# First SwiGLU products of a transformer trunk: four of seven products chained through one PSUM bank, two products issued with 512-column matmuls

## The chip, the cores and the metric

One core of a Trainium2 chip runs the kernel. Its five engines run their own instruction streams and wait for each other through semaphores: PE (matmuls, with weight loads shown as PEld), DVE (VectorE), ACT (ScalarE), POOL (GpSimd, here mostly an issuer of transfers) and SP (another issuer of transfers). The metric is the time of one execution in device microseconds; lower is better.

## The reference

Two layers, each with two SwiGLU blocks around a token mixer. What the change touches is the first product of each SwiGLU block (and the sums of its input), four blocks in all:

```python
D_MODEL, SEQ, DEPTH, D_FF = 1024, 512, 2, 2816

def swiglu(x, w13, w2):
    a, b = jnp.split(x @ w13, 2, axis=-1)
    return (jax.nn.silu(a) * b) @ w2

for l in range(DEPTH):
    x = layer_norm(ALPHA * x + 0.5 * swiglu(x, ffn1_w13[l], ffn1_w2[l]), ...)
    x = layer_norm(ALPHA * x + mixer(x, ...), ...)
    x = layer_norm(ALPHA * x + 0.5 * swiglu(x, ffn2_w13[l], ffn2_w2[l]), ...)
```

Everything is float32. The kernel keeps that precision by splitting each operand into a high and a low part (`split`: ACT writes the high part rounded to fp32r, L126; DVE writes the remainder, L127) and issuing three matmuls for each tile: high x high, high x low, low x high.

## The kernel before, in words

`x @ w13` has 22 column tiles of 128 for `a` and 22 for `b`. Tiles k and k + 11 of `a` and of `b` form a "pair" k, and of the 11 pairs ten (0 to 9) are computed by `seven_pairs`. There the 512 tokens are cut into two halves of 256, the 1024 input features into two halves of 512, and the 2 x 2 x 2 block product is done with seven block products in place of eight, on sums of blocks. So there are sums of input blocks (`x_sums`, once for each SwiGLU: s1 to s4) and sums of weight blocks (`PairWeights.sum`, L570, DVE, four for each pair: t, b, c and a are overwritten or filled by sums of the raw blocks a, b, c, d).

A product is 2 column tiles (z) x 4 feature tiles (m) x 3 matmuls = 24 matmuls of 256 columns (L590). `ORDER` lists the seven products: accumulating bank, input block, weight block. The loop over n = 7 * pair + product does, for each n, in this order: the first part of the eviction of product n - 1 from its bank, a weight sum, the split (L126, L127) of the weights of product n + 3, the rest of the eviction, and in pairs 1, 2, 4, 5, 7 and 8 behind product 3 the sums and splits of an earlier pair's results (`activation_sums`, L337 to L341), and then the matmuls of product n. Every ACT and DVE instruction of this is pinned, so each of these two engines gets its instructions in exactly the order of the code; PE's order is set by a scheduler that may move a matmul ahead of another that waits. Below, "heavy" pair means one with `activation_sums`, "light" pair one without.

Each pair has four PSUM banks of 128 x 512, out of eight. Before, they are A, C, E and B. The evictions of `evictions(k, m)` (L603 to L622) hold three ACT copies or Silu out of PSUM, an ACT Silu in SBUF, and seven 512-wide DVE operations.

```python
ORDER = (("A", "A11", "a"), ("C", "s1", "t"), ("A", "A12", "c"), ("E", "s3", "b"), ("B", "s2", "a"),
         ("C", "s4", "d"), ("E", "A22", "c"))
AHEAD = 3
```

Split weights live in ten buffers, five high and low pairs. The rest of a SwiGLU (`Seven.run`, the second product, 512-column matmuls), the mixer and the norms are not changed, except that the sign of the input sum s2 turns and the parts of the sums lie otherwise in memory.

Of the kernel before, what the change touches and what calls it, by code (L numbers as in the profile page):

```python
# [28 lines left out]
F32 = mybir.dt.float32  # L29
F32R = mybir.dt.float32r  # L30
I32 = mybir.dt.int32
AF = mybir.ActivationFunctionType
# [3 lines left out]
P = 128  # L36
# [47 lines left out]
def trunk(ctx: ExitStack, tc, x_in, xt_in, w13, w2, w_in, w_iv, w_br, w_out, ln_g, ln_b, lb_in, hgn, sgg, sgb, sgws,  # L84
# [12 lines left out]
    def bank(name):  # L97
        return psum.tile([P, 512], F32, tag="ps", name=name)
# [21 lines left out]
    def pin(ins):  # L120

        if pinned[0]:
            tc.keep_in_program_order(ins)

    def split(hi, lo, src):
        pin(S.activation(hi, src, AF.Copy))  # L126
        pin(V.tensor_tensor(lo, src, hi.bitcast(F32), op=ALU.subtract))  # L127
# [145 lines left out]
    def quads(name, dtype=F32):  # L273
        return slot(name, dtype).rearrange("p a t -> p (a t)").rearrange("p (q t) -> p q t", q=4)
# [224 lines left out]
    def x_sums(s, gap=X_GAP):  # L499

        lo_t, hi_t = slice(0, 256), slice(256, 512)
        x3 = quads("xs3")
        v = {c: [] for c in ("s1", "s2", "s3", "s4")}
        for q in range(2):
            r, r2 = xr[q], xr[q + 2]
            v["s1"].append(r[:, :, hi_t])
            v["s2"].append(r2[:, :, hi_t])
            v["s3"].append(x3[:, 2 * q:2 * q + 2])
            v["s4"].append(r2[:, :, lo_t])
            V.tensor_tensor(v["s3"][q], r[:, :, lo_t], r[:, :, hi_t], op=ALU.subtract)  # L510
            V.tensor_tensor(v["s1"][q], r[:, :, hi_t], r2[:, :, hi_t], op=ALU.subtract)
        firsts = [xr[q][:, :, lo_t] for q in range(2)]

        def parts(c):
            s[c] = tuple(quads(f"x{c}{z}", F32R) for z in "hl")
            for q in range(2):
                split(s[c][0][:, 2 * q:2 * q + 2], s[c][1][:, 2 * q:2 * q + 2], v[c][q])

        parts("s1")
        yield 0.0, gap  # L520
        parts("s3")
        for q in range(2):
            V.tensor_tensor(v["s2"][q], firsts[q], v["s1"][q], op=ALU.subtract)
        yield 0.0, gap
        parts("s2")
        for q in range(2):
            V.tensor_tensor(v["s4"][q], v["s4"][q], v["s2"][q], op=ALU.subtract)
        yield 0.0, gap
        parts("s4")


    ORDER = (("A", "A11", "a"), ("C", "s1", "t"), ("A", "A12", "c"), ("E", "s3", "b"), ("B", "s2", "a"),
             ("C", "s4", "d"), ("E", "A22", "c"))
    AHEAD = 3

    class PairWeights:
# [35 lines left out]
    def seven_pairs(seven, s, ks, weights_of, first, due):  # L572


        half = slice(0, 256), slice(256, 512)
        movs = {"A11": lambda m: (xh[m // 2][:, m % 2, half[0]], xl[m // 2][:, m % 2, half[0]]),
                "A12": lambda m: (xh[2 + m // 2][:, m % 2, half[0]], xl[2 + m // 2][:, m % 2, half[0]]),
                "A22": lambda m: (xh[2 + m // 2][:, m % 2, half[1]], xl[2 + m // 2][:, m % 2, half[1]])}
        for c in s:
            movs[c] = lambda m, c=c: (s[c][0][:, m], s[c][1][:, m])  # L580

        def product(ps, units, c, first):
            for z in range(2):
                hi, lo = units[0][:, z], units[1][:, z]
                for m in range(4):
                    ms = slice(m * P, (m + 1) * P)
                    mh, ml = movs[c](m)
                    for i, (a, v) in enumerate(((hi, mh), (hi, ml), (lo, mh))):
                        start = first and z == 0 and m == 0 and i == 0
                        PE.matmul(ps[:, half[z]], a[:, ms], v, start=start, stop=(m == 3 and i == 2),  # L590
                                  skip_group_check=not (first and z == 0))
                    flow.tick(3 * 120.0)

        pws = {ks[0]: first}
        at = lambda n: (ks[n // 7], n % 7)
        last = 7 * len(ks)
        banks = {}

        def evictions(k, m):
            b, r = banks[k], seven.room(k).rearrange("p q t -> p (q t)")  # L600
            lower, upper = r[:, 0:512], r[:, 512:1024]
            if m == 0:
                pin(S.activation(upper, b["A"], AF.Copy))  # L603
            elif m == 2:
                pin(S.activation(lower, b["A"], AF.Silu))
            elif m == 1:
                b["b1"] = wk.tile([P, T], F32, tag="sa", name="b1", bufs=NSA)
                pin(S.activation(b["b1"], b["C"], AF.Copy))
            elif m == 3:
                pin(V.tensor_tensor(b["b1"], b["b1"], b["E"], op=ALU.subtract))  # L610
            elif m == 4:
                pin(V.tensor_tensor(upper, upper, b["B"], op=ALU.subtract))
                pin(V.tensor_tensor(b["b1"], b["b1"], upper, op=ALU.subtract))
            elif m == 5:
                b0 = wk.tile([P, T], F32, tag="sa", name="b0", bufs=NSA)
                pin(V.tensor_tensor(b0, b["C"], upper, op=ALU.subtract))
                pin(V.tensor_tensor(lower, lower, b0, op=ALU.mult))
            elif m == 6:
                pin(V.tensor_tensor(upper, b["E"], upper, op=ALU.add))
                yield  # L620
                pin(S.activation(upper, upper, AF.Silu))
                pin(V.tensor_tensor(upper, upper, b["b1"], op=ALU.mult))  # L622

        for n in range(last):
            k, m = at(n)
            nk = at(n + 7)[0] if n + 7 < last else None
            if m == 0 and nk is not None:
                pws[nk] = weights_of(nk)
                pws[nk].load_d()
            elif m == 1 and nk is not None:  # L630
                pws[nk].load_c()
            ev = evictions(*at(n - 1)) if n else iter(())
            next(ev, None)
            if m == 0:
                banks[k] = {c: bank(f"f{c}{k}") for c in "ABCE"}
                pws[k].sum("a", "a", "b")
            elif m == 1:
                pws[k].sum("c", "a", "c")
            elif m == 2 and nk is not None:
                pws[nk].sum("t", "a", "b")  # L640
            elif m == 3 and nk is not None:
                pws[nk].sum("b", "d", "b")
            if n + AHEAD < last:
                pws[at(n + AHEAD)[0]].split()
            for _ in ev:
                pass
            if m == 3:
                for v in due.get(k, ()):
                    seven.activation_sums(v)
            c, mov, _ = ORDER[m]  # L650
            product(banks[k][c], pws[k].parts[m], mov, c == "B" or m in (0, 1, 3))
        for _ in evictions(*at(last - 1)):
            pass

# [7 lines left out]
    def ffn(l, i, first, next_weights):  # L662
# [38 lines left out]
        def first_weights():  # L701
            pinned[0] = True
            bufs.extend(slot(f"r{v}") for v in ("t", "c0", "c1"))
            pw = weights_of(by_seven[0])
            pw.load_c()
            pw.load_d()
            pw.sum("t", "a", "b")
            for _ in range(AHEAD):
                pw.split()
            pw.sum("b", "d", "b")  # L710
            pinned[0] = False
            return pw

# [11 lines left out]
        else:  # L725
# [6 lines left out]
            for z, j in enumerate(js):  # L732
                pair_of(j, first[z], 256, 256)
                glu(j, first[z])
                if z == 0:
# [2 lines left out]
        seven.home[by_seven[2]] = (xl[0][:, 0, 256:512], xl[0][:, 1, 256:512], xh[0][:, :, 256:512], xh[1][:, :, 256:512])  # L738

        hold = small("hold")  # L740
        tc.keep_in_program_order(G.tensor_scalar(hold, s["s4"][1].bitcast(F32)[:, 3, 255:256], 1.0, 0.0,
                                                 op0=ALU.mult, op1=ALU.add))
        in_dram = flow.add(seven.sums_in_dram(order))
        pinned[0] = True
# [34 lines left out]
    def mixer(l, lb, om, first, next_weights):  # L779
# [17 lines left out]
        def two_tokens():  # L797
# [3 lines left out]
            for k in ks:  # L801
                for name, q, ts in (("A11", k // 2, lo_t), ("A12", 2 + k // 2, lo_t), ("A22", 2 + k // 2, hi_t)):
                    ops[name, k] = xh[q][:, k % 2, ts], xl[q][:, k % 2, ts]
                for name in ("s1", "s2", "s3", "s4"):
                    ops[name, k] = s[name][0][:, k], s[name][1][:, k]
            s.clear()
            A, B, C = ([bank(f"{v}{tt}") for tt in range(2)] for v in ("iA", "iB", "iC"))
            u, p5 = (wk.tile([P, 2, 512], F32, tag="rs", name=v, bufs=2) for v in ("iu", "ip5"))
# [6 lines left out]
            for ps, p in ((A, P1), (B, P6), (C, P5)):  # L815
                for tt in range(2):
                    mm(ps, p, ks[-2:], tt, True, True)
                    if ps is A:
                        S.activation(u[:, tt], A[tt], AF.Copy)
                    elif ps is B:  # L820
                        V.tensor_tensor(u[:, tt], u[:, tt], B[tt], op=ALU.subtract)
                    else:
                        S.activation(p5[:, tt], C[tt], AF.Copy)
            for k in ks:
# [461 lines left out]
```

## Time and profile before

| what | value |
|---|---|
| median of 3 runs | 2036.38 us (2035.0 to 2036.6) |
| profiled execution, first to last instruction | 2033.5 us |
| what the runs have beyond that span (median) | 2.9 us |
| PE busy | 2022.2 us, 12880 matmuls |
| DVE busy | 1639.4 us (81%) |
| ACT busy | 996.8 us (49%) |
| the four `seven_pairs` stages | 201.48, 201.48, 201.87 and 201.48 us |

An engine's busy time is the union of its records. Records of one engine overlap a little, because an instruction is fed in while the one before drains; the pace of an engine is therefore read from the starts of its records, and when a result is ready from the end of a record.

### The profile page before, as it was taken

The numbers are of one execution on the slowest core, as the hardware profiler recorded it, in microseconds if no ns is written. First come the engines' busy times: TensorE is split into PE (matmuls) and PEld (weight loads), VectorE is DVE, ScalarE is ACT, GpSimd is POOL, SyncE is SP. The second block draws the span as 40 slices with busy tenths as digits, with TensorE's granted clock in tenths as the row PEclk, the third lists the DMA queues.
The fourth block names the chain that finished last, engine by engine and source line by source line (L and its number), as shares of the span: only waits on it lengthen the run. The fifth ranks groups of instructions, "written<-read, shape, count | busy, mean of one in ns | idle before, by whom it ended". The sixth has DMA issues, their size and how long they took to land. (4 is left out here: it accounts for less than half of the span.)

```text
span 2033.5 us, 33362 instructions
## 1 busy us (share of the span) xinstructions
PE 2022.2 (99%) x12880; PEld 1840.6 (91%) x12880; DVE 1639.4 (81%) x2453; ACT 996.8 (49%) x1438; POOL 370.5 (18%) x478
## 2 busy tenths in 40 slices
PE   9999999999999999999999999999999999999998
PEld 8999988888888999998899999898888889999986
DVE  8999988956436799999789999889564467999986
ACT  6544665336323554556555456662353235444563
POOL 2322002301000143210132320032010002323101
PEclk9999999999999999999999999999999999999999
DMA  6999777735243289988649997776352433999873
GB/s 233 257 258 238 239 253 238 153 110 181 83 154 115 105 234 241 226 258 269 203 153 271 253 243 242 256 231 137 118 175 83 145 114 113 255 239 230 264 258 129
DMA packets 167550, 404.60 MB, mean 199 GB/s; under 512 B 18880, under 2 KB 19008, under 8 KB 167392
## 3 DMA queue, kind: packets, MB, share of 16 engines
q1 hardware_dynamic: 113472, 261.22, 38.2%
q0 software_dynamic: 53920, 141.26, 29.5%
q8 instruction: 101, 1.65, 0.3%
q14 instruction: 57, 0.47, 0.1%
HBM read 380.38 MB, written 131.07 MB: 252 GB/s over the span
## 5 line engine op out<-in xcount | busy, mean ns | idle before, releaser
L307 POOL DMA_DIRECT2D t<-in_w_dram x176 | 145.5, 901 | 219.5 <-DMA t<-in_w_dram 103.1
L127 DVE TENSOR_TENSOR l_pc<-rc,h_pc 128x1024 fp32r<-128x1024 f32 x80 | 97.8, 1222 | 19.0 <-ACT h_pc L126 19.0
L307 POOL DMA_DIRECT2D t<-t x104 | 56.7, 545 | 288.2 <-DMA t<-in_w_dram 258.6
L155 PE MATMUL z<-xh,h_z 128*128 128x512 f32 x256 | 103.2, 403 | 0.0
L155 PE MATMUL z<-xh,l_z 128*128 128x512 f32 x256 | 99.9, 390 | 0.0
L155 PE MATMUL z<-xl,h_z 128*128 128x512 f32 x256 | 99.9, 390 | 0.0
L127 DVE TENSOR_TENSOR l_pa<-ra,h_pa 128x1024 fp32r<-128x1024 f32 x80 | 97.7, 1221 | 0.0
L126 ACT ACTIVATE h_pc<-rc 128x1024 fp32r<-128x1024 f32 x80 | 84.0, 1050 | 21.0 <-PE fB L590 20.0
L186 POOL TENSOR_SCALAR rstd<-ssq 128x1 f32<-128x1 f32 x24 | 19.3, 803 | 406.8 <-ACT sq L211 406.8
L590 PE MATMUL fA<-xh,h_pc 128*128 128x256 f32 x320 | 90.8, 284 | 0.1
L590 PE MATMUL fC<-xs1h,l_pt 128*128 128x256 f32 x320 | 90.7, 283 | 0.0
L590 PE MATMUL fB<-xs2l,h_pa 128*128 128x256 f32 x320 | 90.7, 283 | 0.0
L590 PE MATMUL fC<-xs1l,h_pt 128*128 128x256 f32 x320 | 90.7, 283 | 0.0
L590 PE MATMUL fB<-xs2h,h_pa 128*128 128x256 f32 x320 | 90.7, 283 | 0.0
L590 PE MATMUL fC<-xs4l,h_pd 128*128 128x256 f32 x320 | 90.7, 283 | 0.0
L590 PE MATMUL fE<-xs3l,h_pb 128*128 128x256 f32 x320 | 90.7, 283 | 0.0
L590 PE MATMUL fB<-xs2h,l_pa 128*128 128x256 f32 x320 | 90.7, 283 | 0.0
L590 PE MATMUL fE<-xh,l_pc 128*128 128x256 f32 x320 | 90.7, 283 | 0.0
L590 PE MATMUL fA<-xh,l_pa 128*128 128x256 f32 x320 | 90.7, 283 | 0.0
L590 PE MATMUL fC<-xs4h,l_pd 128*128 128x256 f32 x320 | 90.7, 283 | 0.0
L590 PE MATMUL fE<-xs3h,l_pb 128*128 128x256 f32 x320 | 90.7, 283 | 0.0
L590 PE MATMUL fC<-xs4h,h_pd 128*128 128x256 f32 x320 | 90.7, 283 | 0.0
(411 smaller groups left out, 7561.6 us busy)
## 6 DMA issues: line engine op xcount, KB each, us to landing
t<-in_w_dram POOLq DMA_DIRECT2D x88, 512.0 KB, 8.8
t<-t POOLq DMA_DIRECT2D x104, 256.0 KB, 5.5
r_d<-t SPq DMA_DIRECT2D x104, 256.0 KB, 4.2
t<-in_w_dram POOLq DMA_DIRECT2D x88, 256.0 KB, 7.1
r_c<-in_w_dram SPq DMA_DIRECT2D x44, 512.0 KB, 4.8
ra<-in_w_dram SPq DMA_DIRECT2D x80, 256.0 KB, 6.0
rb<-in_w_dram SPq DMA_DIRECT2D x80, 256.0 KB, 7.2
rc<-in_w_dram SPq DMA_DIRECT2D x80, 256.0 KB, 7.7
```

Source lines behind the costliest of these rows:

```text
L126: pin(S.activation(hi, src, AF.Copy))
L127: pin(V.tensor_tensor(lo, src, hi.bitcast(F32), op=ALU.subtract))
L155: PE.matmul(ps[:, n0:n0 + n], a[:, cs], m[:, n0:n0 + n], start=(i == 0), stop=(i == 3 * nk - 1))
L186: G.tensor_scalar(r, ssq, inv, eps, op0=ALU.mult, op1=ALU.add)
L307: tc.keep_in_program_order(nc.gpsimd.dma_start(*of(k), **kw))
L590: PE.matmul(ps[:, half[z]], a[:, ms], v, start=start, stop=(m == 3 and i == 2), skip_group_check=not (first and z == 0))
```

## The change

It has four parts.

- The products come in the order A11, s1, s2, s4, s3, A12, A22. Four of them (A11, s2, s3, A22) accumulate in one bank X, which is never restarted inside a pair: after each of the four it is read, and the next adds to it. So c11, c12, c22 and c21 are read from X at successive points of one chain. The sign of s2 is turned for that.
- The two products s1 and s4 accumulate in two banks C (one for each z). For each tile a 256-column matmul of the low weights and one 512-column matmul of the high weights replace three 256-column matmuls: high and low part of the input lie side by side in SBUF (`s[c]` is laid out so), and the high x high and high x low results land in the two halves of the bank. The halves are added when the bank is evicted.
- A12 has a bank A of its own. A pair still has four banks.
- The evictions are written anew, and the weight sums move: c is summed at product 3 (before: 1), t at 4 (before: 2), b at 5 (before: 3), a at 6 of the pair ahead (before: 0 of the pair itself).

```diff
-    ORDER = (("A", "A11", "a"), ("C", "s1", "t"), ("A", "A12", "c"), ("E", "s3", "b"), ("B", "s2", "a"),
-             ("C", "s4", "d"), ("E", "A22", "c"))
+    ORDER = (("X", "A11", "a"), ("C", "s1", "t"), ("X", "s2", "a"), ("C", "s4", "d"), ("X", "s3", "b"),
+             ("A", "A12", "c"), ("X", "A22", "c"))
...
+        def wide(ps, units, c, first):
+
+            for z in range(2):
+                hi, lo = units[0][:, z], units[1][:, z]
+                for m in range(4):
+                    ms = slice(m * P, (m + 1) * P)
+                    v = s[c][m // 2][:, m % 2]
+                    PE.matmul(ps[z][:, 0:256], lo[:, ms], v[:, 0], start=first and m == 0, stop=False,
+                              skip_group_check=True)
+                    PE.matmul(ps[z], hi[:, ms], v.rearrange("p z t -> p (z t)"), start=False, stop=(m == 3),
+                              skip_group_check=True)
+                    flow.tick(120.0 + 227.0)
...
         def evictions(k, m):
-            b, r = banks[k], seven.room(k).rearrange("p q t -> p (q t)")
-            lower, upper = r[:, 0:512], r[:, 512:1024]
+
+            b, r = banks[k], seven.room(k)
+            X, C, A = b["X"].rearrange("p (z t) -> p z t", z=2), b["C"], b["A"].rearrange("p (z t) -> p z t", z=2)
+            c12, c22 = r[:, 0:2], r[:, 2:4]
             if m == 0:
-                pin(S.activation(upper, b["A"], AF.Copy))
+                b["c11"] = wk.tile([P, 2, 256], F32, tag="sa", name="c11", bufs=NSA)
+                pin(S.activation(b["c11"], X, AF.Copy))
+            elif m == 1:
+                for z in range(2):
+                    pin(S.activation(c22[:, z], C[z][:, 256:512], AF.Copy))
+                for z in range(2):
+                    pin(V.tensor_tensor(c22[:, z], c22[:, z], C[z][:, 0:256], op=ALU.add))
             elif m == 2:
...
+                pin(S.activation(c12, X, AF.Copy))
             elif m == 3:
-                pin(V.tensor_tensor(b["b1"], b["b1"], b["E"], op=ALU.subtract))
+                for z in range(2):
+                    for y in range(2):
+                        pin(V.tensor_tensor(c12[:, y], C[y][:, 256 * z:256 * z + 256], c12[:, y],
+                                            op=ALU.add if z else ALU.subtract))
             elif m == 4:
...
+                pin(V.tensor_tensor(c22, c22, X, op=ALU.subtract))
             elif m == 5:
...
+                pin(V.tensor_tensor(b["c11"], b["c11"], A, op=ALU.add))
+                yield
+                pin(S.activation(b["c11"], b["c11"], AF.Silu))
+                pin(V.tensor_tensor(c12, c12, b["c11"], op=ALU.mult))
             elif m == 6:
-                pin(V.tensor_tensor(upper, b["E"], upper, op=ALU.add))
+                c21 = wk.tile([P, 2, 256], F32, tag="sa", name="c21", bufs=NSA)
+                pin(S.activation(c21, X, AF.Silu))
                 yield
-                pin(S.activation(upper, upper, AF.Silu))
-                pin(V.tensor_tensor(upper, upper, b["b1"], op=ALU.mult))
+                pin(V.tensor_tensor(c22, c22, c21, op=ALU.mult))
...
             if m == 0:
-                banks[k] = {c: bank(f"f{c}{k}") for c in "ABCE"}
-                pws[k].sum("a", "a", "b")
-            elif m == 1:
+                banks[k] = {"X": bank(f"fX{k}"), "C": [bank(f"fC{k}{z}") for z in range(2)], "A": bank(f"fA{k}")}
+            elif m == 3:
                 pws[k].sum("c", "a", "c")
-            elif m == 2 and nk is not None:
+            elif m == 4 and nk is not None:
                 pws[nk].sum("t", "a", "b")
-            elif m == 3 and nk is not None:
+            elif m == 5 and nk is not None:
                 pws[nk].sum("b", "d", "b")
+            elif m == 6 and nk is not None:
+                pws[nk].sum("a", "a", "b")
...
-            product(banks[k][c], pws[k].parts[m], mov, c == "B" or m in (0, 1, 3))
+            (wide if c == "C" else product)(banks[k][c], pws[k].parts[m], mov, m in (0, 1, 5))
```

How the instructions stand. In the rows, `h_p` and `l_p` with a letter are the high and low part of a weight block, `ra` to `rd` and `rt` the raw blocks and sums, `r` the results of a pair, `f` with a letter a PSUM bank; the number behind a name tells buffers apart.

DVE in the second SwiGLU, before the change, from the last eviction of one pair to product 3 of the next:

```order
L619 TENSOR_TENSOR r_7561<-fE_7527,r_7561 128x512
L570 TENSOR_TENSOR ra_7514<-ra_7514,rb_7515 128x1024
L127 TENSOR_TENSOR l_pb_7779<-rb_7515,h_pb_7778 128x1024
L622 TENSOR_TENSOR r_7561<-r_7561,b_7595 128x512
L570 TENSOR_TENSOR rc_6933<-ra_7514,rc_6933 128x1024
L127 TENSOR_TENSOR l_pa_7814<-ra_7514,h_pa_7813 128x1024
L570 TENSOR_TENSOR rt<-ra_7763,rb_7764 128x1024
L127 TENSOR_TENSOR l_pd_7848<-rd_7520,h_pd_7847 128x1024
L570 TENSOR_TENSOR rb_7764<-rd_7769,rb_7764 128x1024
L127 TENSOR_TENSOR l_pc_7878<-rc_6933,h_pc_7877 128x1024
L610 TENSOR_TENSOR b_7844<-b_7844,fE_7776 128x512
```

Behind each sum (L570) stands the low part of another block; between a sum and the low part of the summed block stand at least three other DVE instructions. DVE after the change, the same engine and stage, products 0 to 3 of one pair (first piece) and products 4 to 6 (second piece):

```order
L127 TENSOR_TENSOR l_pb_7433<-rb_7142,h_pb_7432 128x1024
L624 TENSOR_TENSOR r_7429<-r_7429,fC_7395 128x256
L624 TENSOR_TENSOR r_7429<-r_7429,fC_7396 128x256
L127 TENSOR_TENSOR l_pc_7460<-rc_6822,h_pc_7459 128x1024
L570 TENSOR_TENSOR rc_6822<-ra_7141,rc_6822 128x1024
L127 TENSOR_TENSOR l_pc_7490<-rc_6822,h_pc_7489 128x1024
L337 TENSOR_TENSOR s_7493<-r_6963 128x256
```

```order
L570 TENSOR_TENSOR rt<-ra_7383,rb_7384 128x1024
L127 TENSOR_TENSOR l_pa_7529<-ra_7383,h_pa_7528 128x1024
L633 TENSOR_TENSOR r_7429<-r_7429,fX_7394 128x512
L570 TENSOR_TENSOR rb_7384<-rd_7389,rb_7384 128x1024
L127 TENSOR_TENSOR l_pt_7559<-rt,h_pt_7558 128x1024
L635 TENSOR_TENSOR c_7430<-c_7430,fA_7397 128x512
L570 TENSOR_TENSOR ra_7383<-ra_7383,rb_7384 128x1024
L127 TENSOR_TENSOR l_pa_7589<-ra_7383,h_pa_7588 128x1024
L638 TENSOR_TENSOR r_7429<-r_7429,c_7430 128x512
L127 TENSOR_TENSOR l_pd_7637<-rd_7389,h_pd_7636 128x1024
L643 TENSOR_TENSOR r_7429<-r_7429,c_7630 128x512
```

The sums of c (`rc`) and of a (`ra`) now stand directly ahead of the low part of that same sum (`l_pc` from `rc`, the second `l_pa` from `ra`), whose high part ACT must write in between. ACT after the change, around product 6 of the pair before that:

```order
L126 ACTIVATE h_pa_7353<-ra_7141 128x1024
L637 ACTIVATE c_7191<-c_7191 128x512
L641 ACTIVATE c_7392<-fX_7152 128x512
L126 ACTIVATE h_pd_7398<-rd_7147 128x1024
L619 ACTIVATE c_7430<-fX_7394 128x512
L126 ACTIVATE h_pb_7432<-rb_7142 128x1024
```

Two evictions (L637, L641) now stand between the high part of the summed a and that of d. PE after the change, at the seam of those two pairs (`fX_7152` is X of the one, `fX_7394` X of the next):

```order
L603 MATMUL fA_7155<-xl_6317,h_pc_7217 128x256
L603 MATMUL fA_7155<-xh_6316,l_pc_7218 128x256
L603 MATMUL fX_7394<-xh_6310,h_pa_7290 128x256
L603 MATMUL fX_7394<-xl_6311,h_pa_7290 128x256
L603 MATMUL fX_7394<-xh_6310,l_pa_7291 128x256
L603 MATMUL fX_7394<-xh_6310,h_pa_7290 128x256
L603 MATMUL fX_7394<-xl_6311,h_pa_7290 128x256
L603 MATMUL fX_7394<-xh_6310,l_pa_7291 128x256
L603 MATMUL fX_7394<-xh_6312,h_pa_7290 128x256
L603 MATMUL fX_7394<-xl_6313,h_pa_7290 128x256
L603 MATMUL fX_7152<-xh_6314,h_pc_7247 128x256
L603 MATMUL fX_7152<-xl_6315,h_pc_7247 128x256
```

Eight matmuls of the next pair's first product were moved ahead of the last product of the pair (24 matmuls on `fX_7152`); the other sixteen follow it. Before the change no product was cut.

More of the change, by code (lines that the diff above doesn't have):

```diff
@@ L514, in parts @@
         def parts(c):
-            s[c] = tuple(quads(f"x{c}{z}", F32R) for z in "hl")
+            s[c] = [slot(f"x{c}{q}", F32R).rearrange("p m (z t) -> p m z t", z=2) for q in range(2)]
             for q in range(2):
-                split(s[c][0][:, 2 * q:2 * q + 2], s[c][1][:, 2 * q:2 * q + 2], v[c][q])
+                split(s[c][q][:, :, 0], s[c][q][:, :, 1], v[c][q])
         parts("s1")
@@ L522, in x_sums @@
         for q in range(2):
-            V.tensor_tensor(v["s2"][q], firsts[q], v["s1"][q], op=ALU.subtract)
+            V.tensor_tensor(v["s2"][q], v["s1"][q], firsts[q], op=ALU.subtract)
         yield 0.0, gap
@@ L526, in x_sums @@
         for q in range(2):
-            V.tensor_tensor(v["s4"][q], v["s4"][q], v["s2"][q], op=ALU.subtract)
+            V.tensor_tensor(v["s4"][q], v["s4"][q], v["s2"][q], op=ALU.add)
         yield 0.0, gap
         parts("s4")
-    ORDER = (("A", "A11", "a"), ("C", "s1", "t"), ("A", "A12", "c"), ("E", "s3", "b"), ("B", "s2", "a"),
-             ("C", "s4", "d"), ("E", "A22", "c"))
+    ORDER = (("X", "A11", "a"), ("C", "s1", "t"), ("X", "s2", "a"), ("C", "s4", "d"), ("X", "s3", "b"),
+             ("A", "A12", "c"), ("X", "A22", "c"))
     AHEAD = 3
@@ L579, in seven_pairs @@
         for c in s:
-            movs[c] = lambda m, c=c: (s[c][0][:, m], s[c][1][:, m])
+            movs[c] = lambda m, c=c: tuple(s[c][m // 2][:, m % 2, z] for z in range(2))
+        def wide(ps, units, c, first):
[9 more added lines that the diff above has]
+                    flow.tick(120.0 + 227.0)
         def product(ps, units, c, first):
@@ L604, in evictions @@
             elif m == 2:
-                pin(S.activation(lower, b["A"], AF.Silu))
-            elif m == 1:
-                b["b1"] = wk.tile([P, T], F32, tag="sa", name="b1", bufs=NSA)
-                pin(S.activation(b["b1"], b["C"], AF.Copy))
+                pin(S.activation(c12, X, AF.Copy))
             elif m == 3:
-                pin(V.tensor_tensor(b["b1"], b["b1"], b["E"], op=ALU.subtract))
+                for z in range(2):
+                    for y in range(2):
+                        pin(V.tensor_tensor(c12[:, y], C[y][:, 256 * z:256 * z + 256], c12[:, y],
+                                            op=ALU.add if z else ALU.subtract))
@@ L611, in evictions @@
             elif m == 4:
-                pin(V.tensor_tensor(upper, upper, b["B"], op=ALU.subtract))
-                pin(V.tensor_tensor(b["b1"], b["b1"], upper, op=ALU.subtract))
+                pin(V.tensor_tensor(c22, c22, X, op=ALU.subtract))
             elif m == 5:
-                b0 = wk.tile([P, T], F32, tag="sa", name="b0", bufs=NSA)
-                pin(V.tensor_tensor(b0, b["C"], upper, op=ALU.subtract))
-                pin(V.tensor_tensor(lower, lower, b0, op=ALU.mult))
+                pin(V.tensor_tensor(b["c11"], b["c11"], A, op=ALU.add))
@@ L634, in seven_pairs @@
             if m == 0:
-                banks[k] = {c: bank(f"f{c}{k}") for c in "ABCE"}
-                pws[k].sum("a", "a", "b")
-            elif m == 1:
+                banks[k] = {"X": bank(f"fX{k}"), "C": [bank(f"fC{k}{z}") for z in range(2)], "A": bank(f"fA{k}")}
+            elif m == 3:
                 pws[k].sum("c", "a", "c")
-            elif m == 2 and nk is not None:
+            elif m == 4 and nk is not None:
                 pws[nk].sum("t", "a", "b")
-            elif m == 3 and nk is not None:
+            elif m == 5 and nk is not None:
                 pws[nk].sum("b", "d", "b")
+            elif m == 6 and nk is not None:
+                pws[nk].sum("a", "a", "b")
             if n + AHEAD < last:
@@ L707, in first_weights @@
             pw.sum("t", "a", "b")
-            for _ in range(AHEAD):
-                pw.split()
+            pw.split()
             pw.sum("b", "d", "b")
+            pw.split()
+            pw.sum("a", "a", "b")
+            pw.split()
             pinned[0] = False
@@ L740, in ffn @@
         hold = small("hold")
-        tc.keep_in_program_order(G.tensor_scalar(hold, s["s4"][1].bitcast(F32)[:, 3, 255:256], 1.0, 0.0,
+        tc.keep_in_program_order(G.tensor_scalar(hold, s["s4"][1].bitcast(F32)[:, 1, 1, 255:256], 1.0, 0.0,
                                                  op0=ALU.mult, op1=ALU.add))
@@ L804, in two_tokens @@
                 for name in ("s1", "s2", "s3", "s4"):
-                    ops[name, k] = s[name][0][:, k], s[name][1][:, k]
+                    ops[name, k] = tuple(s[name][k // 2][:, k % 2, z] for z in range(2))
             s.clear()
@@ L820, in two_tokens @@
                     elif ps is B:
-                        V.tensor_tensor(u[:, tt], u[:, tt], B[tt], op=ALU.subtract)
+                        V.tensor_tensor(u[:, tt], u[:, tt], B[tt], op=ALU.add)
                     else:
```

## The prediction

> **What bounds the kernel now.** I read the page's first section, then what PE waited for, then the four `seven_pairs` stages by themselves.
>
> ```profile
> PE 2022.2 (99%) x12880; PEld 1840.6 (91%) x12880; DVE 1639.4 (81%) x2453; ACT 996.8 (49%) x1438; POOL 370.5 (18%) x478
> ```
> ```profile
> PE idle L1150 <- DVE zero L1147: 1.1, 1, 1.1
> PE pE L366 <- DVE l_d L127: 0.6, 1, 0.6
> PE pb L1179 <- ACT h_b L126: 0.3, 1, 0.3
> ```
> ```profile
> core 0: us, PE busy (x) PEld busy (x) DVE busy (x) ACT busy (x) POOL busy (x), PEclk, DMA share, GB/s
> 29.25:230.73 201.48, 201.48 (x1681) 201.47 (x1680) 188.87 (x226) 101.01 (x127) 57.27 (x67) 1.00 0.89 239
> 707.47:908.95 201.48, 201.48 (x1682) 201.48 (x1681) 189.53 (x227) 100.50 (x127) 57.34 (x67) 1.00 0.90 239
> 1040.89:1242.76 201.87, 201.73 (x1682) 201.53 (x1680) 190.69 (x228) 100.97 (x128) 57.33 (x67) 1.00 0.88 239
> 1718.06:1919.54 201.48, 201.48 (x1681) 201.48 (x1680) 189.44 (x227) 100.50 (x127) 57.30 (x67) 1.00 0.89 239
> ```
>
> The waits of PE are 2 us in all: PE's issue rate is the time. In a stage 1680 matmuls take 201.48 us, 0.120 us each, 20.16 us for a pair (7 x 24). But DVE is busy 189 of those 201 us, so it has about 12 us left in each stage, 1.2 for a pair. Whoever lengthens DVE's chain by more makes DVE the bound. So I need DVE's pace, from one heavy pair and its follower, in order of time:
>
> ```profile
> 703.56 1.22 DVE L570 TENSOR_TENSOR rt<-ra,rb 128x1024 f32<-128x1024 f32 x1
> ...
> 788.91 1.22 DVE L570 TENSOR_TENSOR ra<-ra,rb 128x1024 f32<-128x1024 f32 x1
> 790.05 1.22 DVE L127 TENSOR_TENSOR l_pb<-rb,h_pb 128x1024 fp32r<-128x1024 f32 x1
> 791.18 0.69 DVE L622 TENSOR_TENSOR r<-r,b 128x512 f32<-128x512 f32 x1
> 791.78 1.22 DVE L570 TENSOR_TENSOR rc<-ra,rc 128x1024 f32<-128x1024 f32 x1
> 792.92 1.22 DVE L127 TENSOR_TENSOR l_pa<-ra,h_pa 128x1024 fp32r<-128x1024 f32 x1
> ...
> 798.52 1.23 DVE L127 TENSOR_TENSOR l_pc<-rc,h_pc 128x1024 fp32r<-128x1024 f32 x1 [0.52 <-ACT h_pc L126]
> 799.66 0.42 DVE L337 TENSOR_TENSOR s<-r 128x256 f32<-128x256 f32 x1
> 800.12 0.42 DVE L338 TENSOR_TENSOR s<-r,s 128x256 f32<-128x256 f32 x1
> 800.46 0.42 DVE L127 TENSOR_TENSOR tl<-r,th 128x256 fp32r<-128x256 f32 x1
> 800.79 0.42 DVE L340 TENSOR_TENSOR r<-r 128x256 f32<-128x256 f32 x1
> ...
> 802.19 0.68 DVE L610 TENSOR_TENSOR b<-b,fE 128x512 f32<-128x512 f32 x1
> 802.79 1.22 DVE L127 TENSOR_TENSOR l_pa<-ra,h_pa 128x1024 fp32r<-128x1024 f32 x1
> 803.93 0.68 DVE L612 TENSOR_TENSOR r<-r,fB 128x512 f32<-128x512 f32 x1
> 804.64 0.69 DVE L613 TENSOR_TENSOR b<-b,r 128x512 f32<-128x512 f32 x1
> ...
> 808.85 0.68 DVE L619 TENSOR_TENSOR r<-fE,r 128x512 f32<-128x512 f32 x1
> ```
> ```profile
> 796.95 0.60 ACT L605 ACTIVATE r<-fA 128x512 f32<-128x512 f32 x1 [1.33 <-PE fA L590]
> 797.44 1.05 ACT L126 ACTIVATE h_pc<-rc 128x1024 fp32r<-128x1024 f32 x1
> 801.11 1.04 ACT L126 ACTIVATE h_pa<-ra 128x1024 fp32r<-128x1024 f32 x1
> 802.06 1.04 ACT L126 ACTIVATE h_pt<-rt 128x1024 fp32r<-128x1024 f32 x1
> 809.57 0.63 ACT L621 ACTIVATE r<-r 128x512 f32<-128x512 f32 x1 [2.99 <-DVE r L619]
> ```
>
> Columns are start and length. From start to start DVE takes 1.135 us for 1024 columns (788.91, 790.05, 791.18), 0.60 for 512 (791.18 to 791.78), 0.335 for 256 (800.46 to 800.79). A result read by the very next DVE instruction costs 0.12 more (803.93 to 804.64). The six instructions of `activation_sums` take 2.53 (799.66 to 802.19). ACT takes 0.95 for 1024 columns (801.11 to 802.06), 0.49 for 512. A hand-over between the two takes 0.03 us behind the end of the record: h_pc ends at 798.49, l_pc starts at 798.52; L619 ends at 809.53, L621 starts at 809.57.
>
> DVE before: 11 wide instructions (7 splits, 4 sums) x 1.135 = 12.49, 7 x 0.60 = 4.20, 2 x 0.12 = 0.24: 16.9 us for a light pair, 19.5 for a heavy one, both under PE's 20.16. That fits PE never waiting.
>
> **PE's part of the change.** The pace of a 512-column matmul with a new weight load is seen in the second product:
>
> ```profile
> 298.65 0.39 PE L366 MATMUL pA<-h_c,s 128*128 128x512 f32 x1
> ...
> 301.82 0.39 PE L366 MATMUL pC<-l_c,s 128*128 128x512 f32 x1
> ```
>
> 14 steps in 3.17 us, 0.2265 each. Three 256-column matmuls cost 0.360, the new 256 + 512 cost 0.120 + 0.227 = 0.347; 13 ns less. There are 2 products x 8 = 16 such groups in a pair, 160 in a stage, 640 in all: 2.1 us a stage, 8.3 us in all, and a pair goes from 20.16 to 19.95. The columns streamed are the same; only a per-instruction cost goes. [...]
>
> **DVE's part.** The count of work does not change: 11 x 1.135, four 512-wide (L633, L635, L638, L643) 2.40, six 256-wide (L624 twice, L630 four times) 6 x 0.335 = 2.01: 16.9 again. What changes is the order. The sums of c and of a stand directly ahead of their own low part. From the sum's start: 1.22 for the sum, 0.03, 1.05 for the high part on ACT, 0.03, so the low part starts 2.33 behind the sum in place of 1.135: DVE idles 1.2 us, twice in a pair, and since it works strictly in the pinned order, nothing fills that. A third, small hole: behind the high part of a, ACT runs L637, L641 and then the high part of d (0.95 + 0.49 + 0.49 + 1.05 + 0.03 = 3.01 from its start), while DVE needs l_pa and L638 (1.05 + 0.03 + 1.135 + 0.60 = 2.82): 0.2. So DVE's chain is 16.9 + 2.4 + 0.2 = 19.5 us in a light pair, 22.0 in a heavy one, against 19.95 on PE.
>
> The price of a 256-wide DVE add from PSUM is in no row. Nearest:
>
> ```profile
> L612 DVE TENSOR_TENSOR r<-r,fB 128x512 f32<-128x512 f32 x10 | 6.8, 683 | 2.1 <-PE fB L590 2.1
> L617 DVE TENSOR_TENSOR r<-r,b 128x512 f32<-128x512 f32 x10 | 6.9, 691 | 0.3
> L337 DVE TENSOR_TENSOR s<-r 128x256 f32<-128x256 f32 x8 | 3.4, 419 | 0.0
> ```
>
> At 512 columns PSUM (L612, 683 ns) costs no more than SBUF (L617, 691), so I take the SBUF pace 0.335 for 256. Below it stands half of a 512-wide step, 0.30; above it a step as long as a whole record, 0.42; the full 0.60 of a 512-wide one is the outermost bound. [...]
>
> **Who waits.** The splits run three products ahead and five weight buffers exist, so DVE may be late by a little. From the end of product 4, DVE still has to do the low part of the next pair's a and L633 (X for product 6), while PE has only A12 (2.88 us) and then needs that low part for the eight matmuls moved forward. On time, DVE needs 0.2 + 4 x 0.335 + 1.135 + 1.22 = 3.9 us from the end of product 3 to the end of l_pa, and PE gives it two products, 5.76; of the 1.9 between, the hole behind c takes some 0.7 ahead of L630. A light pair (19.5) wins back 0.45, a heavy one (22.0) loses 2.05. So in every heavy pair PE waits at the moved matmuls.
>
> Sum for a stage: six heavy pairs x 2.05 = 12.3; less 0.45 for each of pairs 0, 3 and 6, light ones ahead of a heavy one, 1.35; that leaves 10.95.
>
> The start adds something. DVE begins the first sum t at 703.56, PE the first product at 707.47. The new order puts l_pa, four 512-wide steps and the sum of b ahead of l_pt: 703.56 + 2 x 1.135 + 4 x 0.60 + 1.135 = 709.4, ready at 710.6, needed at 710.35, 0.26 late; product s1 then ends at 713.4. The sum of a follows at 710.5; ACT can write its high part from 711.75, then that of d, and only then copy c11 out of X: 711.75 + 0.95 + 0.95 + 0.60 = 714.25, 0.9 behind what product s2 wants. Together 1.15 us. The last pair has no sums for a next one, so DVE catches up and the second product starts as before.
>
> 10.95 + 1.15 - 2.1 = +10.0 us a stage, +40 us for four. Against the profiled 2033.5 that is 2073.5; runs stand 2.9 above the span (median 2036.38), so **2076 us**.
>
> Costed at nothing: ACT's six evictions in place of four per pair (100 of 201 us busy); the input sums' new layout and sign (same counts and widths); loads, which are issued at the same products and now needed later; POOL's transfers, which wait for no engine of this loop. If DVE became shorter than PE, the next thing late would be c11 on ACT at the start.
>
> **The rivals.**
>
> 1. The 8.3 us arrive and DVE never holds PE: 2036.4 - 8.3 = **2028**. For it: DVE now has 12 us idle in a stage, and holes might fall into that idle time. Against it: two holes of 1.2 take 24 us of a stage, and the trace shows no slack of that size behind a heavy pair. It decides if a heavy pair's chain is under 19.95, 2.05 less than I count.
> 2. The change is paid for by the gain: start loss and one short wait of about 1 us in each stage, 2036.4 - 8.3 + 4 x 2 = **2036**. That needs a heavy chain near 20.1.
> 3. The bubbles cost less than counted, since a wait of PE also lets ACT and the loads get ahead; only the second of two heavy pairs in a row (2, 5, 8) makes PE wait: 3 x 2.05 + 1.15 - 2.1 = 5.2 a stage, **2057**.
> 4. The one bank X is the wait: c11 and c12 on ACT and L633 on DVE must each be out of X within one other product (2.8 to 2.9 us) or PE stops, in light pairs too. At 1 us for each of 40 pairs on top of my sum: **2116**. By the rows, ACT needs 0.2 + 0.6 us behind the product if it is not queued, so c11 and c12 have 2 us left; the trace speaks against it.
>
> **How the numbers follow.** Chances: forecast 0.75 (2060 to 2098), rival 1 0.09, rival 2 0.03, rival 3 0.08, rival 4 0.05. Range of the forecast: with 0.30 for a narrow add a heavy pair loses 1.84 and a light one wins 0.66, without the start loss 6 x 1.84 - 3 x 0.66 - 2.1 = 7.0 a stage, 2064. With 0.42 a heavy pair loses 2.56 and a light one 0.06 (6 x 2.56 + 3 x 0.06 + 1.15 - 2.1 = 14.6), 2095. Down to rival 3 the range is 2056 to 2096; with 0.60 for a narrow add it would be 2130, which I leave outside. A measurement tells no less than 0.2% (4 us) from no change: faster 0.09, same 0.03, slower 0.88.
>
> **What the changed profile would show.** PE's waits: some 6 of 1.5 to 2 us in each stage, at the first product's matmuls on `fX` right behind those on `fA`, released by DVE `l_pa`; none in light pairs. DVE: idle of about 1.2 us ahead of the `l_pc` behind `rc` and the `l_pa` behind `ra`, released by ACT. Stages of about 211.5 us; the `wide` groups at 0.347 between waits. I am wrong if those idle times are there and PE does not wait (the slack was larger), if PE waits at L633 or c12 (rival 4), or if narrow adds pace at something other than 0.335.

## The result, and the profile after

The changed kernel takes 2091.43 us (median of 4 runs, 2088.66 to 2093.18) where the kernel before takes 2035.81 (4 runs beside them): ratio 1.0274, 95% interval 1.026 to 1.0289. It is slower by 55.6 us. The profiled executions have spans of 2089.7 and 2033.5 us.

Busy time of the engines of the changed kernel, and what PE waited for (total us, times, longest):

```profile
PE 2035.9 (97%) x12240; PEld 1818.3 (87%) x12240; DVE 1645.0 (79%) x2573; ACT 1010.5 (48%) x1518; POOL 336.3 (16%) x478
```
```profile
PE fX L603 <- DVE l_pa L127: 38.5, 24, 2.0
PE fX L603 <- ACT c L619: 1.6, 3, 0.5
PE fC L589 <- DVE l_pt L127: 1.5, 3, 1.1
```

PE issues 640 matmuls fewer and DVE's busy time is nearly what it was (1639.4 before), yet a new wait has come: 24 times, six in each of the four stages, PE stops at the next pair's first product until DVE has written the low part of a. The four stages by themselves:

```profile
core 0: us, PE busy (x) PEld busy (x) DVE busy (x) ACT busy (x) POOL busy (x), PEclk, DMA share, GB/s
28.84:241.87 213.03, 202.03 (x1522) 193.39 (x1521) 188.99 (x250) 103.83 (x146) 49.35 (x67) 1.00 0.84 223
718.77:935.31 216.54, 207.02 (x1523) 197.88 (x1522) 190.51 (x252) 105.05 (x146) 48.43 (x67) 0.98 0.83 220
1067.67:1283.17 215.50, 203.96 (x1523) 194.92 (x1522) 191.27 (x253) 105.08 (x147) 49.40 (x67) 0.99 0.83 221
1758.70:1975.20 216.50, 206.95 (x1523) 197.85 (x1522) 190.50 (x252) 105.03 (x146) 48.39 (x67) 0.98 0.81 219
```

Before they were 201.48 to 201.87; they have grown by 55.3 us together (861.6 beside 806.3), so the whole loss lies here. A stage has the same work each time, but they differ: the first is 213.0 at a clock of 1.00, the others 215.5 to 216.5 at 0.98 and 0.99. Here are the waits in the order in which they fall, in the first stage and then in the second (start, length, operation, and in brackets the idle time ahead):

```profile
68.28 0.39 PE L603 MATMUL fX<-xh,l_pa 128*128 128x256 f32 x1 [1.82 <-DVE l_pa L127]
90.55 0.39 PE L603 MATMUL fX<-xh,l_pa 128*128 128x256 f32 x1 [1.96 <-DVE l_pa L127]
132.53 0.38 PE L603 MATMUL fX<-xh,l_pa 128*128 128x256 f32 x1 [1.62 <-DVE l_pa L127]
154.80 0.39 PE L603 MATMUL fX<-xh,l_pa 128*128 128x256 f32 x1 [1.97 <-DVE l_pa L127]
196.80 0.39 PE L603 MATMUL fX<-xh,l_pa 128*128 128x256 f32 x1 [1.65 <-DVE l_pa L127]
219.06 0.39 PE L603 MATMUL fX<-xh,l_pa 128*128 128x256 f32 x1 [1.97 <-DVE l_pa L127]
...
759.08 0.39 PE L603 MATMUL fX<-xh,l_pa 128*128 128x256 f32 x1 [1.45 <-DVE l_pa L127]
781.34 0.39 PE L603 MATMUL fX<-xh,l_pa 128*128 128x256 f32 x1 [1.96 <-DVE l_pa L127]
823.92 0.39 PE L603 MATMUL fX<-xh,l_pa 128*128 128x256 f32 x1 [0.72 <-DVE l_pa L127]
846.18 0.39 PE L603 MATMUL fX<-xh,l_pa 128*128 128x256 f32 x1 [1.96 <-DVE l_pa L127]
888.75 0.39 PE L603 MATMUL fX<-xh,l_pa 128*128 128x256 f32 x1 [0.72 <-DVE l_pa L127]
911.01 0.39 PE L603 MATMUL fX<-xh,l_pa 128*128 128x256 f32 x1 [1.96 <-DVE l_pa L127]
```

They come in twos, for the two heavy pairs in a row, 22.27 us apart (68.28 to 90.55): that is the length of a heavy pair now. Why, DVE's timeline shows, from the seam of one pair to that of the next, in the second stage:

```profile
822.64 1.22 DVE L127 TENSOR_TENSOR l_pa<-ra,h_pa 128x1024 fp32r<-128x1024 f32 x1
...
827.24 1.22 DVE L570 TENSOR_TENSOR ra<-ra,rb 128x1024 f32<-128x1024 f32 x1
829.67 1.23 DVE L127 TENSOR_TENSOR l_pa<-ra,h_pa 128x1024 fp32r<-128x1024 f32 x1 [1.21 <-ACT h_pa L126]
...
836.42 1.23 DVE L570 TENSOR_TENSOR rc<-ra,rc 128x1024 f32<-128x1024 f32 x1
838.77 1.23 DVE L127 TENSOR_TENSOR l_pc<-rc,h_pc 128x1024 fp32r<-128x1024 f32 x1 [1.13 <-ACT h_pc L126]
...
842.45 1.41 DVE L630 TENSOR_TENSOR r<-fC,r 128x256 f32<-128x256 f32 x4
843.77 1.22 DVE L570 TENSOR_TENSOR rt<-ra,rb 128x1024 f32<-128x1024 f32 x1
844.90 1.22 DVE L127 TENSOR_TENSOR l_pa<-ra,h_pa 128x1024 fp32r<-128x1024 f32 x1
846.04 0.68 DVE L633 TENSOR_TENSOR r<-r,fX 128x512 f32<-128x512 f32 x1
```

DVE goes once round in 22.26 us (822.64 to 844.90), with two holes, 1.21 ahead of the `l_pa` of the summed a and 1.13 ahead of the `l_pc` of the summed c. The four narrow adds of L630 take 1.32 together (842.45 to 843.77), 0.33 each. The first low part of the next a ends at 846.12, and the waiting matmul starts at 846.18.

What PE does behind that wait is the part that I had not forecast. PE's timeline, and the stretch cut into three windows:

```profile
843.94 0.28 PE L603 MATMUL fX<-xl,h_pa 128*128 128x256 f32 x1
846.18 0.39 PE L603 MATMUL fX<-xh,l_pa 128*128 128x256 f32 x1 [1.96 <-DVE l_pa L127]
...
846.74 0.41 PE L603 MATMUL fX<-xh,l_pa 128*128 128x256 f32 x1
846.96 0.41 PE L603 MATMUL fX<-xh,h_pa 128*128 128x256 f32 x1
847.17 0.41 PE L603 MATMUL fX<-xl,h_pa 128*128 128x256 f32 x1
...
849.93 0.28 PE L603 MATMUL fX<-xh,h_pc 128*128 128x256 f32 x1
850.05 0.28 PE L603 MATMUL fX<-xl,h_pc 128*128 128x256 f32 x1
```
```profile
843.90:846.50 2.60, 0.64 (x5) 0.44 (x4) 2.60 (x3) 1.06 (x1) 0.67 (x2) 1.00 1.08 332
846.50:849.92 3.42, 3.42 (x18) 3.42 (x17) 3.42 (x5) 0.00 (x0) 1.16 (x2) 0.50 0.87 305
849.92:853.00 3.08, 3.08 (x28) 3.08 (x27) 1.88 (x2) 2.16 (x4) 1.11 (x3) 1.00 0.82 159
```

From 846.50 on the granted clock is 0.50 and a step is 0.213 us (846.74 to 846.96 to 847.17) in place of 0.12; 3.42 us later the clock is back at 1.00. There are seven such stretches in the four stages (0, 3, 1 and 3), each of about 3.41 us and each behind a wait of nearly 2 us; the stage without one is the short one.

### The profile page after: what moved, and what is told of

It is laid out like the page before. It is cut to its first block, busy times and chain, and to the rows that moved or that the text cites. A ratio compares the mean times of both kernels' runs of the same rounds, so it can differ in the third digit from the quotient of the medians.

```text
span 2089.7 us, 32071 instructions
## 1 busy us (share of the span) xinstructions
PE 2035.9 (97%) x12240; PEld 1818.3 (87%) x12240; DVE 1645.0 (79%) x2573; ACT 1010.5 (48%) x1518; POOL 336.3 (16%) x478
## 5 line engine op out<-in xcount | busy, mean ns | idle before, releaser
L603 PE MATMUL fX<-xh,l_pa 128*128 128x256 f32 x320 | 93.7, 293 | 38.5 <-DVE l_pa L127 38.5
L603 PE MATMUL fX<-xs,h_pa 128*128 128x256 f32 x640 | 117.1, 283 | 1.6 <-ACT c L619 1.6
L603 PE MATMUL fX<-xs,h_pb 128*128 128x256 f32 x640 | 116.7, 283 | 0.0
L591 PE MATMUL fC<-xs,h_pd 128*128 128x512 f32 x320 | 115.0, 399 | 0.0
L591 PE MATMUL fC<-xs,h_pt 128*128 128x512 f32 x320 | 114.7, 398 | 0.0
L603 PEld LDWEIGHTS fX<-xs,h_pa 128*128 128x128 f32 x640 | 102.0, 191 | 4.2 <-ACT c L619 2.6
L603 PEld LDWEIGHTS fX<-xs,h_pb 128*128 128x128 f32 x640 | 102.3, 191 | 2.1
L603 PE MATMUL fX<-xh,h_pc 128*128 128x256 f32 x320 | 94.7, 296 | 0.0
L603 PE MATMUL fX<-xh,l_pc 128*128 128x256 f32 x320 | 94.6, 296 | 0.0
L603 PE MATMUL fX<-xl,h_pc 128*128 128x256 f32 x320 | 94.5, 295 | 0.0
```

The lines of the kernel that those rows point to most:

```text
L591: PE.matmul(ps[z], hi[:, ms], v.rearrange("p z t -> p (z t)"), start=False, stop=(m == 3), skip_group_check=True)
```

## The experiments

The theory: two sums that stand directly ahead of their own low part make holes in DVE's fixed order, a heavy pair's chain becomes longer than PE's, and PE waits for it. Rivals: the one bank X with its evictions is the wait; the wide matmuls are slow; or the half clock is the main loss. All edits but where said are made on the changed kernel.

**One hole taken away, twice.** The sum of a is moved to one product earlier, behind the sum of b, so that another low part stands between it and its own:

```diff
             elif m == 5 and nk is not None:
                 pws[nk].sum("b", "d", "b")
-            elif m == 6 and nk is not None:
                 pws[nk].sum("a", "a", "b")
```

> The sum of a is taken in product 5 right behind the sum of b, so the low part of t and L635 (1.135 + 0.60 us) stand between it and its own low part. Theory (DVE's holes behind the two sums hold PE): one of two holes of 1.2 us goes, a heavy pair's DVE chain falls from 22.0 to 20.8 us, PE's waits fall from about 2 us to about 1, none is long enough for the half-clock stretches seen behind waits of 2 us; stages near 208 us, the whole near 2061. Rival (the chained bank X holds PE): waits stay at 2 us, 2091.

Measured: 2062.65 us (2 runs), ratio 1.0138 (1.0118 to 1.0158). PE's wait in its profile:

```profile
PE fX L603 <- DVE l_pa L127: 21.7, 24, 1.1
```

The other hole is filled in heavy pairs by putting the six instructions of `activation_sums` between the sum of c and its low part:

```diff
+            if m == 3:
+                for v in due.get(k, ()):
+                    seven.activation_sums(v)
             if n + AHEAD < last:
                 pws[at(n + AHEAD)[0]].split()
-            if m == 3:
-                for v in due.get(k, ()):
-                    seven.activation_sums(v)
```

> In heavy pairs the six instructions of activation_sums stand between the sum of c and its low part (before: behind the low part). Theory: the hole behind c is filled in heavy pairs, their chain falls from 22.0 to about 20.8, PE's waits become 0.2 to 0.8 us, no half-clock stretch; stages near 205 us, the whole near 2050. Rival (X): 2091.

Measured: 2054.04 us (2 runs), ratio 1.0096 (1.0076 to 1.0116).

```profile
PE fX L603 <- DVE l_pa L127: 14.3, 24, 0.8
```

Each hole is a part of the loss, and neither is the whole. The 24 waits stay, shorter, and the mean granted clock of both runs is 0.999: no half-clock stretch is left in either.

**Both holes taken away**, the two edits together.

> Both order changes at once, no work added or left out. Theory: a heavy pair's chain is 19.6 to 19.9 us, under PE's 20.0; PE waits only at the start of each stage (about 1.1 us); stages near 202 us, the whole 2034 to 2040. Rival (X or the 256-wide adds hold PE): waits of 1 us and more remain in heavy pairs, 2060 or above.

Measured: 2034.49 us (10 runs), ratio 0.9997 (0.9988 to 1.0007). What PE waited for, and two of the stages:

```profile
PE fX L603 <- ACT c L619: 1.6, 3, 0.6
PE fC L589 <- DVE l_pt L127: 1.5, 3, 1.1
...
PE pE L366 <- DVE l_d L127: 0.3, 1, 0.3
```
```profile
28.23:229.20 200.97, 200.97 (x1522) 193.15 (x1521) 189.89 (x251) 105.94 (x146) 49.38 (x67) 1.00 0.87 238
705.26:907.05 201.79, 201.00 (x1523) 193.10 (x1522) 190.46 (x252) 106.12 (x146) 48.56 (x67) 1.00 0.88 236
```

All 24 waits are gone, and with them 57 us. The products, banks, evictions and wide matmuls are still those of the change; only two places in the order of the work differ. So the order of those two places is the cause of the loss, and the one bank X is not: what is left at `fX` is three short waits at the starts of stages.

**The clock.** Each of the seven stretches came behind a wait of nearly 2 us. Whether they come when PE is kept busy in that time, this run asks. Sixteen matmuls whose result is dropped (they are written into bank A, which the next product clears) are added ahead of product 5 of each heavy pair; that is 384 matmuls, 46 us of PE's time at 0.12 each:

```diff
+            if m == 5 and k in due:
+                for i in range(16):
+                    PE.matmul(banks[k]["A"][:, half[0]], pws[k].parts[m][0][:, 0, 0:P], movs[mov](0)[0], start=True,
+                              stop=True, skip_group_check=True)
```

> The changed kernel with 16 extra 256-column matmuls in each of the 24 heavy pairs, ahead of product 5 into its bank, which that product then clears: 24 x 16 x 0.120 = 46 us of additional PE work whose result is dropped. Theory: DVE sets the pace there and the half-clock stretches come from PE's pauses of 2 us; the extra work fits into the pauses, these fall to some 0.2 us, the 7 half-clock stretches go: 2091 less up to 10 us, 2080 to 2088. Rival (the half clock or PE itself sets the pace): 2137.

Measured: 2084.51 us (4 runs), ratio 1.0244 (1.0226 to 1.0261): with more work on PE it is 6.9 us faster than the changed kernel by the medians, some 6 us by the two ratios, whose intervals just touch. The mean granted clock of its profile is 0.999, beside 0.993 of the changed kernel. Its first, second and fourth stages:

```profile
29.20:242.60 213.40, 213.25 (x1618) 204.74 (x1617) 189.37 (x250) 104.27 (x146) 49.42 (x67) 1.00 0.82 223
718.35:932.20 213.85, 213.11 (x1618) 204.76 (x1617) 189.81 (x251) 104.40 (x146) 48.54 (x67) 1.00 0.82 223
...
1755.67:1969.50 213.83, 213.04 (x1618) 204.74 (x1617) 189.80 (x251) 104.39 (x146) 48.48 (x67) 1.00 0.83 222
```

The first stage, where the changed kernel had no half clock either, stays where it was (213.4 beside 213.0). The second and fourth fall from 216.5 to 213.8. So three stretches of half clock cost a stage some 2.7 us. The steps say the same: three stretches are each 1.5 longer, and the next wait behind two of them is 0.93 shorter (0.72 in place of 1.65), 2.6 in all. And the half clock is not the main loss, since the first stage has none and is still 11.5 us longer than before.

**The start of the stages.** On top of both orders, the first pair's third split is put ahead of the sums of b and a, and one split behind the copy of c11:

```diff
+            pw.split()
             pw.sum("b", "d", "b")
             pw.sum("a", "a", "b")
-            pw.split()
...
-            if n + AHEAD < last:
-                pws[at(n + AHEAD)[0]].split()
+            for i in range(1 if n > 1 else 2 * n):
+                if n + AHEAD < last:
+                    pws[at(n + AHEAD)[0]].split()
```

> Both order changes, and the start of a stage: the split of t ahead of the sums of b and a, and the split of product 3's weights behind the copy of c11 in place of ahead of it. Theory: the start loss (0.3 us at product s1 and 0.9 at s2 in each stage by my count) falls to under 0.3; stages near 200.8 us, 3 us less than both_orders in all, near 2032, and so under the kernel before by about 4 us. Rival (the start loss comes from elsewhere, the input sums): as both_orders, 2034 to 2035.

Measured: 2034.85 us (11 runs), ratio 0.9998 (0.9989 to 1.0007). A miss: the two kinds of start waits are gone, but the time is that of `both_orders`. PE's waits in its profile:

```profile
PE pE L366 <- DVE l_d L127: 0.9, 1, 0.9
PE fX L603 <- DVE l_pa L127: 0.8, 1, 0.8
PE fC L589 <- DVE r L624: 0.7, 1, 0.7
```

Of 3.1 us of waits at the starts, 1.5 has come back as two waits in one stage, and the second product waits 0.6 longer. The rest is in steps too short for this table of waits. Taking all steps of PE in the four stages that are more than 8 ns over the usual step between matmuls of those widths, they add up to 5.3 us over that pace in `both_orders` and still to 4.8 here. What causes the short ones is not shown.

**What the wide matmuls are worth.** In that kernel, each 512-column matmul is written as two of 256:

```diff
-                    PE.matmul(ps[z], hi[:, ms], v.rearrange("p z t -> p (z t)"), start=False, stop=(m == 3),
-                              skip_group_check=True)
+                    for y in range(2):
+                        PE.matmul(ps[z][:, 256 * y:256 * y + 256], hi[:, ms], v[:, y], start=False, stop=(m == 3),
+                                  skip_group_check=True)
```

> As start_too, but each 512-column matmul of the two wide products is two of 256 columns again, into the same two halves of the bank; nothing else differs. It prices the wide matmul where PE sets the pace. At 0.353 us for a pair of 256 and 512, as the trace of the changed kernel has it, 640 x 7 ns = 4.5 us more than start_too; at the 0.347 of the prediction 8.3 us more; at nothing (Rival: the saving is lost elsewhere) the same.

Measured: 2037.6 us (11 runs), ratio 1.0013 (1.0004 to 1.0022), 2.75 us above `start_too` on the same chip. That lies between the 4.5 and the nothing that I had named. Divided by 640 groups it is 4.3 ns a group, a third of what the prediction counted. By its ratio this kernel, with 256-column matmuls alone, is 0.13% slower than the kernel before: the rest of the change still costs a little, and what the wide matmuls save only pays for that. PE's timeline of `start_too` shows part of why the saving is small:

```profile
737.63 0.40 PE L591 MATMUL fC<-xs,h_pd 128*128 128x512 f32 x1
737.87 0.28 PE L589 MATMUL fC<-xs,l_pd 128*128 128x256 f32 x1
...
738.69 0.40 PE L591 MATMUL fC<-xs,h_pd 128*128 128x512 f32 x1
```

Behind a 512-column matmul the 256-column one starts 0.24 later, not 0.227. Three groups take 1.06 us, 0.353 each, where I had 0.347. Over all 640 groups that alone would leave some 4 us of saving; against it stand the longer steps named above, which add up to 4.8 us in `start_too` and to 3.5 in this run.

The same edit on the changed kernel itself, where DVE sets the pace of the heavy pairs:

> The changed kernel with each 512-column matmul of the wide products as two of 256 again, nothing else. Theory (DVE sets the pace in heavy pairs, so a saving on PE is lost in the next wait, and the half-clock stretches hang on pauses of 2 us): PE has 3 to 4 us more work in all, its pauses become 0.1 us shorter, the time stays within 3 us of 2091 or falls by a few us if half-clock stretches go. Rival (the time follows PE's work): 3 to 8 us more, 2094 to 2099.

Measured: 2092.3 us (4 runs), ratio 1.0277 (1.0263 to 1.0291), beside 1.0274 (1.026 to 1.0289) with the wide matmuls. Where PE waits for DVE, a faster PE brought nothing that was measured. By the time alone 3 to 4 us more is not excluded, since each interval is 3 us to either side. The waits say more clearly where the added work went: PE waited 34.4 us for `l_pa` in this profile, 38.5 with the wide matmuls. This profile also has nine half-clock stretches in place of seven.

**Like beside like.** To get more of the saving, `start_too` with the four low matmuls of a half first and the four wide ones behind them:

```diff
                     flow.tick(120.0)
+                for m in range(4):
+                    ms = slice(m * P, (m + 1) * P)
+                    v = s[c][m // 2][:, m % 2]
...
-                    flow.tick(120.0 + 227.0)
+                    flow.tick(227.0)
```

> As start_too, but in a wide product the four 256-column matmuls of the low weights come first for each z, then the four 512-column ones. In the trace of start_too the step from a 512-column matmul to a 256-column one takes 0.236 us where 512 to 512 takes 0.227. Theory (that step costs what is missing from the saving): a wide product has 2 such steps in place of 8, 6 x 9 ns less less what 256 to 512 gains back (0.1175 against 0.120), 80 products: 2 to 4 us less, 2031 to 2033 beside start_too's 2035. Rival (the 512-column matmul is simply slower into these banks): no change.

Measured: 2033.46 us (11 runs), ratio 0.9991 (0.9982 to 1.0). By the ratios that is 1.4 us below `start_too`, short of the 2 to 4 that I expected, and the two intervals overlap. PE's timeline, with four matmuls in a row each:

```profile
735.96 0.63 PE L589 MATMUL fC<-xs,l_pd 128*128 128x256 f32 x4
736.43 1.09 PE L595 MATMUL fC<-xs,h_pd 128*128 128x512 f32 x4
737.36 0.40 PE L607 MATMUL fX<-xs,h_pb 128*128 128x256 f32 x2
```

Four 256-column steps take 0.47, four 512-column steps 0.93, or 0.233 each. In a row they are a little faster than alternating (0.350 a group in place of 0.353), but not the 0.227 of the second product's; so the rival has a part in it, though why they are slower here is not shown. This is the fastest version that I ran, and its interval against the kernel before just reaches 1: a gain of up to 0.2%, or none.

## Why the prediction was right, and where its sizes were off

I said 2076 us (2056 to 2096) and slower with 0.88; it is 2091.43. The step-by-step sum over four stages, forecast beside measured:

| term | forecast | measured |
|---|---|---|
| waits for `l_pa` in heavy pairs | +43.8 | +42.3 |
| starts of stages | +4.6 | +4.1 |
| wide matmuls and fewer steps | -8.3 | about -2.2 |
| half clock | none | about +10.5 |
| sum | +40 | +54.7 |

The measured waits are the profile's idle time plus 0.16 for each, because a record of 0.28 us hides the next start, which would have come 0.12 behind: 38.5 + 24 x 0.16 = 42.3, and 1.6 + 1.5 + 6 x 0.16 = 4.1. The last two come from the steps between starts in the trace: all steps at the trace's shortest pace would be 8.7 below before, and 6.5 of that is lost again to longer steps around wide matmuls and right behind waits; the steps of the seven half-clock stretches are 10.5 longer than at full clock. The four stages grew by 55.3; 0.6 of that is not placed.

That 42.3 came so near to 43.8 is in part luck. Five of the 24 waits come behind a half-clock stretch and are 0.72 in place of 1.65, 4.6 us less together; without the half clock the waits would be 46.9. The half clock's own cost is then 10.5 less 4.6, or 5.9, near the 6 to 7 us that `more_matmuls` took away.

- **DVE's holes.** Right. Holes of 1.21 and 1.13 where I said 1.2; a heavy chain of 22.26 where I said 22.0. Taking both away took away every heavy wait (`both_orders`), so this is shown, not only argued.
- **Who waits, and where.** Right. Six in a stage, at the moved matmuls on `fX`, 19 of them 1.45 to 1.97 where I said 1.5 to 2, none in light pairs. The other five are the 0.72 behind a half-clock stretch: PE comes later by itself.
- **Narrow adds.** Right: 0.33 from PSUM, beside 0.335 in the SBUF rows.
- **The start.** Right in size (4.1 of 4.6), but not in place: I counted 1.15 in every stage, and the first stage has none, the second and fourth 1.1 each and the third 1.9. Taking it away brought nothing measurable (`start_too`), so it is a wait that I can show and not a gain that I can show.
- **The wide matmuls.** Mis-sized. "13 ns less" took the pace of 512-column matmuls that follow each other and put it beside 256-column ones. Alternating, a group costs 0.353, and the whole saving is 2.75 us instead of 8.3. In the changed kernel, where DVE sets the pace of the heavy pairs, none of it could be measured (`changed_256`).
- **The half clock.** Missing from the sum. I priced a wait at its own length. `more_matmuls` shows that the trouble behind a wait is a cost of its own: 6 to 7 us less with the waits filled.
- **Rivals.** Rival 1 (no wait) and rival 2 (one short wait in each stage) fell with the 24 waits. Rival 3 (only the second of two heavy pairs waits) fell too: both wait. Rival 4 (bank X) fell with `both_orders`, which keeps that bank and has no wait in light pairs. The range held the time because its upper end, set for a slower narrow add, was wide enough for an effect that it wasn't made for: that the time fell inside it is partly luck. With 0.60 for a narrow add the prediction's own sum gives 2134, not 2130; nothing hung on it.

## What to carry to other kernels

On an engine that works in a fixed order, look at the distance between an instruction and the one that needs its result through another engine, not only at the sum of busy times: DVE had 12 us to spare in a stage, and two hand-overs that stood too close made DVE idle for about 23 of a stage (10 pairs x 2.34). Here the faster instruction brought a saving where its engine set the pace (2.75 us, `start_too` beside `start_too_256`); where another engine did, none was measured (2091.43 beside 2092.3, `changed_256`). And the price of an instruction should be read from a row where it stands in the same neighbourhood: alternating, a group cost 0.353, where the rows apart had given 0.347. The seven waits on PE of nearly 2 us that had a half clock behind them cost more than their length, 6 to 7 us more together by `more_matmuls`; look at the granted clock right behind a wait.

## What the runs showed of the hardware that I had not expected

The granted clock fell to 0.50 for 3.41 us behind 7 of the 24 waits, none of them over 2.0 us; in the stretch shown above, 2.24 us lay between one matmul's start and the next (843.94 to 846.18). In the profiles with waits of at most 1.1 us (48 of them in `a_early` and `fill_c`) the mean clock was 0.999. The starts of the seven stretches in the trace's record of the clock lie a whole number of 3.413 us apart: 781.65, 846.50 and 911.35 are 64.85 apart, 19 times 3.413, and from the first of the seven to the last it is 343 times.

If marks of that spacing are drawn through the four stages of the changed kernel, the idle time of PE between two marks tells its waits apart. The half clock came behind each of the seven intervals with 1.89 to 1.96 us idle, at the mark that ends the interval, and behind none of the others, which have at most 1.81. In the first stage, which has none, the waits are as long, but the three of 1.96 and 1.97, at 90.55, 154.80 and 219.06, are each cut by a mark, with 1.81, 1.20 and 1.36 us as the larger piece. In `changed_256` the pauses fall elsewhere: its waits for `l_pa` are at most 1.8 us, and there are nine such stretches (mean granted clock 0.991). All this is read from where the pauses happened to fall; no run moved a pause on purpose, and what brings the half clock is not shown.

In `start_too` a step between a 512-column and a 256-column matmul is not the mean of the two kinds: 0.24 behind the wide one and 0.12 behind the narrow one (737.63, 737.87 and 737.99), where a row of wide ones in the second product steps by 0.2265 in the trace before the change.
